# A hybrid attention and retention layer: 96 stores go to ScalarE's queue, gated rows are fetched in two groups, and the retention's projection begins with two first halves

## The chip, the cores and the metric

The kernel runs on one core of a Trainium2 chip. The time is that of one execution on the device in microseconds (us); each kernel is run several times and the median is taken. One execution is also recorded by the hardware profiler. Its span runs from the first to the last instruction. PE is TensorE (PEld its weight loads), DVE is VectorE, ACT is ScalarE, POOL is GpSimd, SP is SyncE, which does nothing here but issue transfers; "SPq" in a row is that queue.

## The reference

One layer of a diffusion backbone over 1024 latent tokens of width 1024 (with 256 context tokens), in fp32. The input is modulated and normalized to `hx`; one input projection feeds a 2-D neighbourhood attention (8 heads of 64), a bidirectional chunkwise retention (4 heads, 128 for queries and keys, 256 for values) and gates. What the change touches comes after both:

```python
def _ret_output(o, g):
    of = o.astype(jnp.float32)
    mu = jnp.mean(of, axis=-1, keepdims=True)
    var = jnp.mean(jnp.square(of - mu), axis=-1, keepdims=True)
    on = ((of - mu) * lax.rsqrt(var + EPS)).astype(o.dtype)
    return _merge_heads(on) * jax.nn.silu(g)

def _merge(o_na, o_ret, gate_na, gate_ret, w_proj_na, w_proj_ret, w_out):
    merged = jax.nn.sigmoid(gate_na) * (o_na @ w_proj_na) + jax.nn.sigmoid(gate_ret) * (o_ret @ w_proj_ret)
    return merged @ w_out
...
x = x + g1 * _merge(o_na, o_ret, xga, xgb, w_proj_na[l], w_proj_ret[l], w_out[l])
x = x + g2 * _conv_ffn(hx2, w_up[l], conv_w[l], conv_b[l], w_down[l])
```

## The kernel before

Every fp32 operand is split in two parts, `hi` (a cast on ScalarE) and `lo` (the source less `hi`, on VectorE), and a product takes three matmuls: hi x hi, hi x lo, lo x hi. Tiles are 128 partitions x 512 elements. Everything is kept transposed: a block `db` of 128 channels stands on the partitions, and the tokens are two halves of 512. The stages follow one another in this order, with their places in the trace: start and modulation (0 to 90 us), neighbourhood attention with the heads' projections (90 to 390), retention (to 720), `pn`, the projection of the attention's output (720 to 774), Gates (774 to 926), `pr`, the projection of the retention's output (929 to 1025), `om`, the output projection (to 1118), and the ConvFFN (to the end).

In neighbourhood attention and retention, some gate products run in between ("filled in"): `gate_fill` copies the product from PSUM to `gs` on ScalarE and stores it to DRAM, `d_gate` (L361). In the retention, `mix_c` transposes a head's output by PE, copies it to `ot` on ScalarE, and stores it to `d_oret` (L1210). In the `pn` stage a product times its gate goes to `pnt` and is stored to `d_pn` (L1509).

The class `Gates` (a seven-product scheme for 2x2 blocks, hence `Seven`) computes the remaining gates. A unit is a retention head ("ret") or a block of merge gates ("merge"). `done` applies the activation to the product on ScalarE, multiplies by the fetched `o` on VectorE (not for the second block of a merge unit), and stores the tile `c` to `d_orr` (the gated rows of retention's output), `d_pn` or `d_gate` (L1487). The units run interleaved, in a list `steps` of pairs (unit, product); each step is 12 matmuls, `u` in the rows. The last unit has ten list places from its own first step, `n0`, to the end.

The gated rows come back from `d_orr` for `pr`: `orr_raw(half, k)` gives the tiles and issues the load of one (k of 8, half of 2), and `split` makes the two parts of it. Their tiles take the places of parts of `hx`, so that a load's split must stand behind the last product that reads that part. Loads that must be split go through `rawload`, which has three buffers named `raw`; split weights have six buffers named `wc`. `merge_load` brings the merge gates and the `pn` products into `sg`; `g = pr * gate + pn` is then split to `mh`, `ml` for `om`.

What sets the order: the framework's scheduler sets the order of each engine's instructions from the program's order and dependencies; `late` and the manual parts pin it. Each engine, and each queue, takes its instructions strictly in this order; all loads and stores of this kernel are issued by SP. A store whose tile isn't ready thus holds the loads behind it.

Of the kernel before, what the change touches and what calls it, by code (L numbers as in the profile page):

```python
# [9 lines left out]
F32R = mybir.dt.float32r  # L10
AF = mybir.ActivationFunctionType
ALU = mybir.AluOpType
# [6 lines left out]
KB = D // P  # L19
# [10 lines left out]
RH = 4  # L30
# [10 lines left out]
def tile_hybrid_layer(ctx, tc: tile.TileContext, io, dbg=None):  # L41
    nc = tc.nc
    vec, act, pool, pe, sync = nc.vector, nc.scalar, nc.gpsimd, nc.tensor, nc.sync
# [41 lines left out]
    def split(hi, lo, src, lo_eng=None):  # L85
        act.copy(hi, src)  # L86
        (lo_eng or vec).tensor_tensor(lo, src, hi.bitcast(F32), ALU.subtract)  # L87
# [28 lines left out]
    def mm_a(out, wcs, hi, lo):  # L116
        for _ in chain(out, wcs, hi, lo):
            pass
# [235 lines left out]
    def gate_fill(p, tag, bufs, g, wg):  # L354
        db, br = g
        for half in range(2):
            m = mm_tile()
            yield from chain(m, wg, hxs(0, half), hxs(1, half), STEP)
            t = p.tile([P, 512], F32, tag=tag, bufs=bufs, name="gs")
            act.copy(t, m)  # L360
            sync.dma_start(d_gate[db * 2 + br, half], t)  # L361
            if half:
                spilled[g] = True
            yield
# [701 lines left out]
    class Head:  # L1066
# [129 lines left out]
        def mix_c(self, n):  # L1196
            tb, o = self.back[n], self.o[n]
            tp = prt.tile([P, 2, P], F32, tag="s", bufs=2, name="tpo")
            for b in range(2):
                pe.transpose(tp[:, b], o[:, b * P : (b + 1) * P], ident)  # L1200
            h = self.h
            end = h == RH - 1 and n >= NTB - 2
            if end:
                ot = wpool.tile([P, 512], F32, tag="raw", bufs=3, name="oe")[:, : 2 * P].rearrange("p (b t) -> p b t", b=2)
            else:
                ot = rt.tile([P, 2, P], F32, tag="ot", bufs=2, name="ot")
            act.copy(ot, tp)
            stores.append((d_oret[2 * h : 2 * h + 2, :, tb * P : (tb + 1) * P].rearrange("b p t -> p b t"), ot))
            if not end:
                sync.dma_start(*stores.pop())  # L1210

    stores = []

# [117 lines left out]
    def g_ps(name):  # L1331
        return pg.tile([P, 512], F32, tag="g", bufs=6, name=name)
# [26 lines left out]
        sync.dma_start(raw, d_onat[n * P : (n + 1) * P])  # L1359
        onr.append(raw)  # L1360
    while stores:
        sync.dma_start(*stores.pop(0))
    for n, raw in enumerate(onr):
        tp = pg.tile([P, NPAIR, P], F32, tag="g", bufs=6, name="tpn")
        for k in range(NPAIR):
# [76 lines left out]
    class Gates(Seven):  # L1442
# [38 lines left out]
        def done(self, b, half, t=None, src=None):  # L1481
            t = self.c[b, half]
            src, n, cs = t if src is None else src, self.n, slice(half * 512, half * 512 + 512)
            act.activation(t, src, AF.Silu if self.kind == "ret" else AF.Sigmoid)
            if self.kind == "ret" or b == 0:
                vec.tensor_tensor(t, t, self.o, ALU.mult)
            sync.dma_start(d_orr[2 * n + b, :, cs] if self.kind == "ret" else d_pn[n, half] if b == 0 else d_gate[2 * n + 1, half], t)  # L1487

    nsp = len(spilled) // 2
    gu = [Gates("ret", h) for h in range(RH)] + [Gates("merge", db) for db in range(nsp, KB)]  # L1490
# [1 line left out]
    for db in range(KB):  # L1492
        if db % 2 == 0:
            hs = hx_sums(db // 2)
            next(hs)
        wp = [wload(io["w_pna"][db, 0])]
        for half in range(2):
            sl_ = slice(half * 512, half * 512 + 512)
            m = g_ps("pn")
            mm_a(m, wp, lambda k: ona[0][:, k, sl_], lambda k: ona[1][:, k, sl_])  # L1500
            t = onap.tile([P, 512], F32, tag="pn", bufs=3, name="pnt")
            if (db, 0) in spilled:
                g = onap.tile([P, 512], F32, tag="sg", bufs=2, name="sgt")
                sync.dma_start(g, d_gate[2 * db, half])
                act.activation(g, g, AF.Sigmoid)
                vec.tensor_tensor(t, m, g, ALU.mult)
            else:
                act.copy(t, m)
            sync.dma_start(d_pn[db, half], t)  # L1509
        if db % 2 == 0:  # L1510
            next(hs)
    gu[0].load()
# [16 lines left out]
    orr = {}  # L1529

    def orr_raw(half, k):
        i, kb = (k // KH if half else 1 - k // KH), k % KH + KH * half
        orr[half, k] = [hxpool.tile([P, 512], F32R, tag=f"{t}{i}{kb}", bufs=1, name="orr") for t in ("high", "low")]
        return orr[half, k], rawload(d_orr[k, :, half * 512 : half * 512 + 512], late)

    gate_sums = down_sums(gr, RET_SUMS, GATE_SUMS)
    steps = interleaved(0, len(gu))
    n0, fetched = steps.index((len(gu) - 1, 0)), None
    for n, (i, k) in enumerate(steps):
        gu[i].step(k)  # L1540
        if n % 3 == 1:
            next(gate_sums, None)
        if fetched:
            split(*fetched[0], fetched[1])
            fetched = None
        if n0 <= n < n0 + 2 * RH:
            fetched = orr_raw(0, n - n0)
    wp0 = [wload(io["w_pret"][0, i]) for i in range(2)]
    for _ in gate_sums:
        pass  # L1550
    gr.release()
# [6 lines left out]
    def gtile(half, dt, name):  # L1558
        return gpool[half].tile([P, 512], dt, tag="g", bufs=2 * KB + 1, name=name)

    sg = {}

    def merge_load(db, halves=(0, 1)):
        for half in halves:
            sg[db, 0, half] = gtile(half, F32, "sg")
            sync.dma_start(sg[db, 0, half], d_pn[db, half])
            sg[db, 1, half] = t = gtile(half, F32, "sg")
            sync.dma_start(t, d_gate[2 * db + 1, half])
            if (db, 1) in spilled:
                act.activation(t, t, AF.Sigmoid)  # L1570
# [8 lines left out]
    pjp = sb("out_sums", "right")  # L1579
    out_sums = down_sums(pjp, GATE_SUMS, NH, 7)  # L1580
    mg = {}
    wp_next = wp0
    for db in range(KB):
        wp = wp_next
        if db == 0:
            merge_load(0, (0,))
            for k in range(2 * RH):
                hl, raw = orr_raw(1, k)
                split(*hl, raw)
            merge_load(0, (1,))  # L1590
        if db + 1 < KB:
            wp_next = [wload(io["w_pret"][db + 1, i]) for i in range(2)]
            merge_load(db + 1)
        if db == 2:
            brow(0, gate1)
        for half in range(2):
            m = g_ps("pr")
            mm_a(m, wp, lambda k: orr[half, k][0], lambda k: orr[half, k][1])
            g = sg[db, 1, half]
            vec.tensor_tensor(g, m, g, ALU.mult)  # L1600
            (vec if db == KB - 1 else pool).tensor_tensor(g, g, sg[db, 0, half], ALU.add)
            h_, l_ = gtile(half, F32R, "mh"), gtile(half, F32R, "ml")
            split(h_, l_, g)
            mg[db, half] = (h_, l_)
            if db > 1:
                next(out_sums, None)
    pjp.release()
    wo = {}
    for kb in range(KB):
# [475 lines left out]
```

## Time and profile before

| | before |
|---|---|
| runs, us | 1777.6, 1780.02, 1781.48 (median 1780.02) |
| span of the profiled execution, us | 1772.4 |
| median of the runs less that span, us | 7.6 |
| PE busy | 1725.5 us, 97% |
| DVE, ACT, POOL busy | 74%, 48%, 32% |
| DMA engines | 44.3% of the span, 262 MB |
| mean granted clock of PE | 0.991 |

The profiled execution's own time isn't listed apart from the runs; its span is, and the runs lie 5.2 to 9.1 us above it. The profile's busy times say how much of the span each engine worked; the trace's rows give an instruction's start, its length, its engine and line, and in brackets the idle time before it and what ended that idle time. A row of waits has the total, the number of times and the longest wait.

### The profile page before, as it was taken

How to read it: one execution, taken by the hardware profiler on the slowest of the kernel's cores; microseconds unless marked ns; L12 is line 12 of the kernel's file. 1: busy time of each engine (PE TensorE's matmuls, PEld its weight loads, DVE VectorE, ACT ScalarE, POOL GpSimd, SP SyncE). 2: the span in 40 equal slices, each digit the busy share in tenths (PEclk: the TensorE clock that was granted, in tenths of full speed). 3: DMA queues.
4: the chain of work that ended last, by engine and by line, in shares of the span. 5: the costliest groups of instructions: out<-in, count | busy, mean ns of one | idle time of the engine just before them, and what ended most of it. 6: DMA issues, size and time to landing. Idle time of an engine off the chain costs nothing.

```text
span 1772.4 us, 24732 instructions
## 1 busy us (share of the span) xinstructions
PE 1725.5 (97%) x8357; PEld 1429.4 (81%) x8357; DVE 1312.3 (74%) x2458; ACT 851.1 (48%) x1833; POOL 570.9 (32%) x477
## 2 busy tenths in 40 slices
PE   8799999999999999999999999999999999999997
PEld 4588888888888888788877888888888888788886
DVE  5978888765776766777655556889899999876755
ACT  5667666652443444443444323454444444554444
POOL 2610000002334343555412400155455555211444
PEclk9899999999999999999999999999999999999999
DMA  9133334432231212677548733742322332586754
GB/s 357 56 113 120 106 113 134 142 110 104 72 108 48 72 39 65 202 243 241 187 168 278 236 127 137 253 147 91 117 90 89 119 119 90 167 297 191 241 167 151
DMA packets 139552, 261.62 MB, mean 148 GB/s; under 512 B 15872, under 2 KB 28320, under 8 KB 139424
## 3 DMA queue, kind: packets, MB, share of 16 engines
q1 hardware_dynamic: 139424, 260.03, 44.3%
q8 instruction: 66, 1.08, 0.3%
q14 instruction: 62, 0.51, 0.1%
HBM read 187.87 MB, written 69.48 MB: 145 GB/s over the span
## 4 chain that ended last, share of the span: by engine, by line
PE 39%; issue 6%; DVE 5%; DMA 3%; POOL 3%; ACT 1%; SPq 0%; POOLq 0%; DVEq 0%; ACTq 0%
PE u L1374 27%; PE y L1374 4%; PE pr L111 2%; PE pr L112 1%; PE pr L110 1%; PE om L123 1%; PE om L122 1%; PE om L121 1%; DMA raw<-d_orr 1%; DVE wc L87 1%; POOL x L1899 0%; DMA uu<-d_t 0%; DMA ur<-in_w_up 0%; DVE b L1350 0%; POOL pd L1936 0%
## 5 line engine op out<-in xcount | busy, mean ns | idle before, releaser
L1374 PE MATMUL u<-T,wc 128*128 128x512 f32 x960 | 225.7, 391 | 0.6 <-ACT pu L1413 0.3
L1374 PE MATMUL y<-wc,ahl 128*128 128x512 f32 x924 | 212.0, 391 | 2.9 <-DVE wc L87 1.8
L1374 PEld LDWEIGHTS u<-T,wc 128*128 128x128 f32 x960 | 179.4, 188 | 41.5 <-ACT pu L1413 4.2
L1374 PEld LDWEIGHTS y<-wc,ahl 128*128 128x128 f32 x924 | 174.4, 189 | 40.2 <-DVE wc L87 2.5
L87 DVE TENSOR_TENSOR wc<-ur,wc 128x512 fp32r<-128x512 f32 x137 | 125.0, 915 | 62.2 <-ACT wc L86 62.2
L86 ACT CAST wc<-ur 128x512 fp32r<-128x512 f32 x137 | 85.1, 622 | 124.3 <-PE y L1374 71.8
L111 PE MATMUL mm<-low,wc 128*128 128x512 f32 (+1 forms) x328 | 124.0, 378 | 0.0
L1374 PE MATMUL u<-h2a,wc 128*128 128x512 f32 x480 | 112.4, 389 | 0.7 <-DVE pu L1422 0.7
L110 PE MATMUL mm<-hx,wc 128*128 128x512 f32 x264 | 107.4, 407 | 0.3 <-DVE vc L221 0.3
L1374 PEld LDWEIGHTS u<-h2a,wc 128*128 128x128 f32 x480 | 90.0, 188 | 19.9 <-DVE pu L1422 1.2
L112 PE MATMUL mm<-hx,wc 128*128 128x512 f32 x264 | 105.1, 398 | 0.0
L86 ACT CAST wc<-s 128x512 fp32r<-128x512 f32 x80 | 49.6, 621 | 89.7 <-PE u L1374 86.9
L123 PE MATMUL mm<-wc,low 128*128 128x512 f32 (+1 forms) x240 | 91.2, 380 | 0.0
L1513 POOL TENSOR_TENSOR col<-col,bcol 128x32 f32<-128x32 f32 x1 | 0.3, 254 | 281.9 <-DVE aw L538 281.9
L1374 PE MATMUL u<-hxT,wc 128*128 128x512 f32 x384 | 89.6, 389 | 0.0
L87 DVE TENSOR_TENSOR wc<-s,wc 128x512 fp32r<-128x512 f32 x80 | 87.3, 1092 | 3.1 <-ACT wc L86 2.6
L1374 PEld LDWEIGHTS u<-hxT,wc 128*128 128x128 f32 x384 | 72.1, 188 | 15.0
L87 DVE TENSOR_TENSOR wc<-raw,wc 128x512 fp32r<-128x512 f32 x92 | 71.4, 784 | 13.3 <-ACT wc L86 13.2
L121 PE MATMUL mm<-wc,hx 128*128 128x512 f32 x192 | 75.2, 392 | 0.6 <-ACT r L1105 0.6
L122 PE MATMUL mm<-wc,hx 128*128 128x512 f32 x192 | 75.2, 392 | 0.0
L86 ACT CAST wc<-raw 128x512 fp32r<-128x512 f32 x92 | 57.0, 622 | 32.3 <-DMA raw<-in_w_up 5.0
L111 PEld LDWEIGHTS mm<-low,wc 128*128 128x128 f32 x328 | 62.1, 189 | 6.9
(393 smaller groups left out, 4695.7 us busy)
## 6 DMA issues: line engine op xcount, KB each, us to landing
ur<-in_w_up SPq DMA_DIRECT2D x80, 256.0 KB, 3.0
ur<-d_a SPq DMA_DIRECT2D x77, 256.0 KB, 3.0
aw<-in_w_ada SPq DMA_DIRECT2D x32, 512.0 KB, 3.3
pj<-in_w_down SPq DMA_DIRECT2D x44, 256.0 KB, 4.9
d_w<-pj SPq DMA_DIRECT2D x44, 256.0 KB, 2.0
d_a<-sa SPq DMA_DIRECT2D x44, 256.0 KB, 2.0
ur<-d_w SPq DMA_DIRECT2D x44, 256.0 KB, 3.5
d_a<-at SPq DMA_DIRECT2D x33, 256.0 KB, 2.7
```

What stands on the lines that cost most here:

```text
L86: act.copy(hi, src)
L87: (lo_eng or vec).tensor_tensor(lo, src, hi.bitcast(F32), ALU.subtract)
L110: pe.matmul(out, wh, xh, start=k == 0, stop=False)
L111: pe.matmul(out, wh, xl, start=False, stop=False)
L112: pe.matmul(out, wl, xh, start=False, stop=k == n - 1)
L121: pe.matmul(out, ah, bh, start=first, stop=False)
L122: pe.matmul(out, ah, bl, start=False, stop=False)
L123: pe.matmul(out, al, bh, start=False, stop=last)
L1374: pe.matmul(out, a, b, start=first and n == 0, stop=last and n == 2, skip_group_check=True)
L1513: pool.tensor_tensor(col[:, 16:48], col[:, 16:48], bcol[:, 16:48], ALU.add)
```

## The change

Three things change. First, the stores of L361, L1210, L1362, L1487 and L1509 (16 + 30 + 2 + 32 + 16 = 96) are issued by ScalarE instead of SP. Second, the gated rows of half 0, which were fetched one by one at the last unit's list places 0 to 7, are fetched at places -6 to -3 (k = 0 to 3) and 1 to 4 (k = 4 to 7), the first two of half 1 at places 7 and 9, and `w_pret` of block 0 is loaded within the last three list places. Third, `pr` runs in the order (0,0), (1,0), (0,1), (1,1), (2,0), (2,1) and on, as (block, half); the weights of block 1 are loaded before the six rows of half 1 that are left.

```diff
             act.copy(t, m)
-            sync.dma_start(d_gate[db * 2 + br, half], t)
+            act.dma_start(d_gate[db * 2 + br, half], t)
...
             if not end:
-                sync.dma_start(*stores.pop())
+                act.dma_start(*stores.pop())
...
     while stores:
-        sync.dma_start(*stores.pop(0))
+        act.dma_start(*stores.pop(0))
...
-            sync.dma_start(d_orr[2 * n + b, :, cs] if self.kind == "ret" else d_pn[n, half] if b == 0 else d_gate[2 * n + 1, half], t)
+            act.dma_start(d_orr[2 * n + b, :, cs] if self.kind == "ret" else d_pn[n, half] if b == 0 else d_gate[2 * n + 1, half], t)
...
-            sync.dma_start(d_pn[db, half], t)
+            act.dma_start(d_pn[db, half], t)
...
-    n0, fetched = steps.index((len(gu) - 1, 0)), None
+    n0, fetched, wp0 = steps.index((len(gu) - 1, 0)), None, []
+    fetches = {d: (k // 8, k % 8) for k, d in enumerate((-6, -5, -4, -3, 1, 2, 3, 4, 7, 9))}
...
-        if n0 <= n < n0 + 2 * RH:
-            fetched = orr_raw(0, n - n0)
-    wp0 = [wload(io["w_pret"][0, i]) for i in range(2)]
+        if n - n0 in fetches:
+            fetched = orr_raw(*fetches[n - n0])
+        if n >= len(steps) - 3 and len(wp0) < 2:
+            wp0.append(wload(io["w_pret"][0, len(wp0)]))
+    split(*fetched[0], fetched[1])
...
-    wp_next = wp0
-    for db in range(KB):
-        wp = wp_next
-        if db == 0:
-            merge_load(0, (0,))
-            for k in range(2 * RH):
+    wps = {0: wp0}
+    merge_load(0, (0,))
+    for n, (db, half) in enumerate(((0, 0), (1, 0), (0, 1), (1, 1), *((db, half) for db in range(2, KB) for half in range(2)))):
+        nx = 1 if n == 0 else db + 1
+        if nx < KB and nx not in wps:
+            wps[nx] = [wload(io["w_pret"][nx, i]) for i in range(2)]
+            if nx > 1:
+                merge_load(nx)
+        if n == 0:
+            for k in range(2, 2 * RH):
                 hl, raw = orr_raw(1, k)
                 split(*hl, raw)
+            merge_load(1)
             merge_load(0, (1,))
```

The order on SP at the end of Gates, before (names are `out<-in` with a running number; `d_orr` loads are the gated rows, `in_w_pret` the weights of `pr`, `o` a fetch for the gates):

```order
L1487 DMA d_pn_62<-c_10135 128x512
L91 DMA raw_10144<-d_orr_63 128x512
L91 DMA raw_10171<-d_orr_63 128x512
L1479 DMA o_10221<-d_pn_62 128x512
L1487 DMA d_gate_61<-c_10162 128x512
L1487 DMA d_pn_62<-c_10190 128x512
L91 DMA raw_10198<-d_orr_63 128x512
L91 DMA raw_10243<-in_w_pret 128x512
L1487 DMA d_gate_61<-c_10215 128x512
L91 DMA raw_10248<-in_w_pret 128x512
L1566 DMA sg_10269<-d_pn_62 128x512
L1568 DMA sg_10271<-d_gate_61 128x512
```

And the same place on SP after the change:

```order
L91 DMA raw_10134<-d_orr_63 128x512
L1479 DMA o_10181<-d_pn_62 128x512
L91 DMA raw_10204<-d_orr_63 128x512
L91 DMA raw_10206<-in_w_pret 128x512
L91 DMA raw_10232<-in_w_pret 128x512
L1479 DMA o_10237<-d_pn_62 128x512
L91 DMA raw_10261<-d_orr_63 128x512
L91 DMA raw_10286<-in_w_pret 128x512
L91 DMA raw_10291<-in_w_pret 128x512
L91 DMA raw_10298<-d_orr_63 128x512
L1569 DMA sg_10281<-d_pn_62 128x512
L1571 DMA sg_10283<-d_gate_61 128x512
```

The stores are gone from it, the weights of two blocks stand ahead of most of half 1's rows, and two of those rows (`raw_10204`, `raw_10261`) stand ahead of block 1's weights.

PE at the end of the first chain of `pr` (24 matmuls), before, and then after:

```order
L112 MATMUL pr_10347<-orr_10196,wc_10250 128x512
L110 MATMUL pr_10378<-orr_10274,wc_10245 128x512
L111 MATMUL pr_10378<-orr_10275,wc_10245 128x512
L112 MATMUL pr_10378<-orr_10274,wc_10245 128x512
L110 MATMUL pr_10378<-orr_10280,wc_10245 128x512
```

```order
L112 MATMUL pr_10347<-orr_10132,wc_10234 128x512
L110 MATMUL pr_10398<-orr_9883,wc_10288 128x512
L111 MATMUL pr_10398<-orr_9884,wc_10288 128x512
L112 MATMUL pr_10398<-orr_9883,wc_10288 128x512
L110 MATMUL pr_10398<-orr_9905,wc_10288 128x512
```

Before, the second chain reads new rows (half 1) with the same weights; after, it reads the rows of half 0 once more, with block 1's weights.

ScalarE in the retention, before, and then after (`ot` is the copy of a head's transposed output, `v` the cast of projected values):

```order
L1125 CAST qk_5448<-tp_5445 128x256
L1207 COPY ot_5454<-tpo_5451 128x256
L1100 CAST v_5463<-mm_5391 128x256
L1134 ACTIVATE kz_5579<-r0_5466,dec_158 128x128
L1156 COPY ds_5489<-dS_5476 128x256
```

```order
L1125 CAST qk_5448<-tp_5445 128x256
L1207 COPY ot_5454<-tpo_5451 128x256
L1210 DMA d_oret_58<-ot_5454 128x2x128
L1100 CAST v_5463<-mm_5391 128x256
L1134 ACTIVATE kz_5579<-r0_5466,dec_158 128x128
```

The store now stands between the copy and the next cast on ScalarE.

More of the change, by code (lines that the diff above doesn't have):

```diff
@@ L1581, in tile_hybrid_layer @@
     mg = {}
-    wp_next = wp0
-    for db in range(KB):
-        wp = wp_next
-        if db == 0:
-            merge_load(0, (0,))
-            for k in range(2 * RH):
+    wps = {0: wp0}
[8 more added lines that the diff above has]
+            for k in range(2, 2 * RH):
                 hl, raw = orr_raw(1, k)
                 split(*hl, raw)
+            merge_load(1)
             merge_load(0, (1,))
[L1591 to L1594, printed above, removed]
+        if (db, half) == (2, 0):
             brow(0, gate1)
[L1596 to L1606, printed above, removed]
+        m = g_ps("pr")
+        mm_a(m, wps[db], lambda k: orr[half, k][0], lambda k: orr[half, k][1])
+        g = sg[db, 1, half]
+        vec.tensor_tensor(g, m, g, ALU.mult)
+        (vec if db == KB - 1 else pool).tensor_tensor(g, g, sg[db, 0, half], ALU.add)
+        h_, l_ = gtile(half, F32R, "mh"), gtile(half, F32R, "ml")
+        split(h_, l_, g)
+        mg[db, half] = (h_, l_)
+        if db > 1:
+            next(out_sums, None)
     pjp.release()
```

## The prediction

> **What bounds the kernel now.** I read the page's totals, then the waits of PE between the retention and the output projection, then PE's row of instructions through that stretch, and last SP's and ScalarE's rows for who makes it wait.
>
> ```profile
> span 1772.4 us, 24732 instructions
> PE 1725.5 (97%) x8357; PEld 1429.4 (81%) x8357; DVE 1312.3 (74%) x2458; ACT 851.1 (48%) x1833; POOL 570.9 (32%) x477
> ```
>
> PE is busy for 97% of the span, so a change that takes no matmul away can win only what PE loses: idle gaps, and matmuls that run slowly after them. The change touches 720 to 1025 us, and PE's waits from 640 to 1040 are these:
>
> ```profile
> PE pr L110 <- ACT wc L86: 2.8, 1, 2.8
> PE pn L112 <- DVE wc L87: 2.2, 2, 1.5
> PE pr L110 <- ACT orr L86: 2.1, 3, 1.3
> PE tpn L1366 <- DVE ona L1369: 2.1, 1, 2.1
> PE pr L111 <- DVE orr L87: 1.4, 4, 0.7
> ```
>
> Three of the five belong to pr, the retention's projection, which waits for splits (the cast on ACT, the difference on DVE) of weights and gated rows: 6.3 us. PE's timeline gives the pace and the gaps:
>
> ```profile
> 904.45 8.32 PE L1374 MATMUL u<-hxT,wc 128*128 128x512 f32 x36
> 912.61 0.39 PE L1374 MATMUL u<-hx,wc 128*128 128x512 f32 x1
> ...
> 925.99 0.39 PE L1374 MATMUL u<-hx,wc 128*128 128x512 f32 x1
> 929.18 0.50 PE L110 MATMUL pr<-orr,wc 128*128 128x512 f32 x1 [2.80 <-ACT wc L86]
> ...
> 931.78 0.63 PE L110 MATMUL pr<-orr,wc 128*128 128x512 f32 x1
> 932.20 0.63 PE L111 MATMUL pr<-orr,wc 128*128 128x512 f32 x1
> ...
> 939.82 0.50 PE L111 MATMUL pr<-orr,wc 128*128 128x512 f32 x1 [0.72 <-DVE orr L87]
> ...
> 944.44 0.50 PE L110 MATMUL pr<-orr,wc 128*128 128x512 f32 x1 [1.27 <-ACT orr L86]
> ...
> 1025.09 0.39 PE L112 MATMUL pr<-orr,wc 128*128 128x512 f32 x1
> 1025.31 0.39 PE L121 MATMUL om<-wo,mh 128*128 128x512 f32 x1
> ```
>
> Undisturbed, 36 matmuls start within 912.61 - 904.45 = 8.16 us, 0.2267 us apart; at 931.78 the step to the next is 0.42. The granted clock explains the slow ones:
>
> ```profile
> 929.20:932.60 3.40, 3.40 (x8) 2.42 (x9) 2.04 (x5) 2.33 (x4) 0.00 (x0) 0.59 0.83 288
> 946.30:949.70 3.40, 3.18 (x7) 2.10 (x8) 2.08 (x4) 1.24 (x2) 0.65 (x1) 0.59 0.72 253
> 949.70:1010.00 60.30, 60.30 (x266) 49.94 (x266) 31.93 (x42) 21.96 (x37) 23.94 (x18) 1.00 0.78 263
> ```
>
> (After the length: busy time and count of PE, PEld, DVE, ACT, POOL, then clock, DMA share and GB/s.) Twice the clock is 0.59 for 3.40 us; from 949.70 PE is full at clock 1.00, so nothing is left to win there, though DMA is at 0.78.
>
> The sum available: from the last Gates matmul (925.99) to the first of the output projection (1025.31) are 99.32 us, and 1 + 384 matmuls (8 blocks x 2 halves x 24) at 0.2267 take 87.3. The excess is **12.05 us**: 6.3 in the eight gaps, 2 x 3.40 x (1 - 0.2267/0.42) = 3.1 by the half clock, and the other 2.6 in slow restarts behind the gaps (0.50 instead of 0.39 long).
>
> Why the rows come late is on SP's row, in the waits of its queue, and in the chain:
>
> ```profile
> 917.64 0.32 SPq L1487 DMA_DIRECT2D d_pn<-c  x1
> 918.06 0.88 SPq L91 DMA_DIRECT2D raw<-d_orr  x2
> ...
> 923.27 0.32 SPq L1487 DMA_DIRECT2D d_pn<-c  x1
> 923.64 0.43 SPq L91 DMA_DIRECT2D raw<-d_orr  x1
> ```
>
> ```profile
> SPq L1487 <- DVE c L1486: 15.3, 5, 4.7
> SPq L91 <- DVE orr L87: 11.1, 9, 2.0
> ```
>
> ```profile
> 916.92 0.70 DVE c L1486
> ...
> 929.24 2.60 DMA raw<-d_orr
> 931.85 0.63 ACT orr L86
> 932.50 0.70 DVE orr L87
> ...
> 940.69 4.85 DMA raw<-d_orr
> ```
>
> Loads of gated rows go out right behind stores that sat at the head of SP's queue until VectorE's product was there: 15.3 us between 890 and 950. (In the chain: a load's way to its landing, 2.60 to 4.85 us, then 0.63 of cast and 0.70 of difference.) Half 0's last load leaves at 923.64 and half 1's eight between 929.24 and 940.69, while pr(0, half 1) would at full pace want them from 934.6 to 939.4 (929.18 + 24 x 0.2267, then 0.68 each).
>
> **The change, part by part.**
>
> *Stores off SP.* 96 issues leave SP; the 64 of the other lines are loaded again only a stage later and free queue time alone, while the 32 of L1487 free the loads behind them, by up to the 4.7 us of the longest wait. The price is that ScalarE now issues them, in order, and its next cast stands behind each.
>
> ```profile
> L1210 SPq DMA_DIRECT2D d_oret<-ot x30: 360/371/386, 475.7 to 711.6; - x30
> ```
>
> ```profile
> L91 SPq DMA_DIRECT2D raw<-in_w_ret x32: 327/328/1362, 315.4 to 601.2; - x32
> ```
>
> ```profile
> 475.26 0.38 ACT L1207 COPY ot<-tpo 128x256 f32<-128x256 f32 x1
> 476.60 0.37 ACT L1100 CAST v<-mm 128x256 fp32r<-128x256 f32 x1 [0.96 <-PE mm L123]
> ```
>
> ```profile
> ACT v L1100 <- PE mm L123: 32.8, 30, 2.7
> ```
>
> In the retention a store of 0.37 follows ot's copy, where ScalarE is idle for 0.96 us until PE delivers mm; from 450 to 700 the cast v waits so 30 times, 1.09 us in the mean: hidden. No row shows an issue from ScalarE; I bound it by 0.36 (SP's fastest for this transfer) and 1.36 (SP's slowest of a load in the same stage), which would cost 30 x (1.36 - 1.09) = 8 us. I take SP's median of 0.37, the same transfer, so 0 on PE. In the attention stage ten stores of d_gate stand between a copy and casts with no gap:
>
> ```profile
> 340.63 1.08 ACT L495 CAST PT<-ptp 128x512 fp32r<-128x512 f32 x2
> ...
> 344.71 0.76 PE L511 MATMUL R<-PT,V 128*128 128x256 f32 x5
> ```
>
> At most 10 x 0.37 = 3.7 us, at least 0. I take 0: the casts end at 341.71 and the product that reads PT starts at 344.71, so 3.0 us, less VectorE's difference of 0.7, cover it. In the Gates stage each store also waits for the product that follows its own activation, 0.70 on VectorE and what is queued there:
>
> ```profile
> ACT wc L86 <- PE u L1374: 45.8, 27, 2.1
> ```
>
> ```profile
> 740.00:775.00 35.00, 33.85 (x148) 27.65 (x149) 33.43 (x40) 17.99 (x34) 15.83 (x10) 1.00 0.64 203
> ```
>
> There ScalarE's weight casts wait 45.8 us (775 to 926) for buffers that PE has not yet freed: they run ahead of PE, and that lead covers 32 stores at 0.37 + 0.70 (34 us, spread over the 151 us of the stage). If the lead were gone, the next late thing would be wc of a Gates product. In the w_pna stage (740 to 775) DVE is busy 33.43 of 35 us and its lateness sets PE's 2.2 us of waits; ScalarE's 16 stores there neither feed nor free DVE: 0, between -2.2 and +1.6 (a half clock from one new gap).
>
> *Gated rows in two groups, w_pret early.* The same 16 + 4 loads, no instruction more. The first four of half 0 come 6 steps before the last unit's first step (2.72 us of 12 matmuls each), the others from one step after, so half 0 is split by the end of Gates instead of the cast at 928. The 2.80 gap at 929.18 goes, with its half clock (1.6) and its restart. The splits, 0.63 on ScalarE and 0.70 on VectorE each, are only moved to earlier steps; ScalarE has the room there (the 45.8 us above).
>
> *Two first halves first.* pr(1, half 0) now stands before pr(0, half 1), 24 x 0.2267 = 5.44 us more until half 1 is wanted. With pr starting at 926.2, pr(1, 0) starts at 931.7 and pr(0, 1) at 937.1; its pairs follow every 0.68 us, the last at 941.9. New is that block 1's weights are wanted at 931.7 instead of at the third chain. Both of its loads go out before the six remaining rows, near 925 (an estimate: behind half 0's last load of before, 923.64, and two issues); with 0.4 of issue, a landing of 2.60 to 4.85 and 1.3 of split the first is ready by 929.3 to 931.6: hidden, barely in the worst case; the second is wanted 2.7 later. The six rows have three buffers, so two rounds of issue 0.4 + landing + 1.3: from 927, 2 x (0.4 + 2.6 + 1.3) = 8.6, or 2 x (0.4 + 4.85 + 1.3) = 13.1, so the last is ready between 935.6 and 940.1, or up to 3 later if SP's interleaved sg loads and one more round of weights stand between (943.1). Need: 941.9. Leftover: 0 to 1.2 us of gap, and with a half clock and a restart up to 3.6. I take 1.0.
>
> A rule to weigh here: "TensorE: Matmul & The Clock Gate" of the Trainium skill, section "What's actually happening", has the clock halved after at least one idle window of about 3.4 us, the windows running freely. The trace agrees with the 3.40 us and half rate, but shows it behind a 2.80 us gap and again behind scattered gaps of 1.27 and less. By the rule a leftover gap of 1.2 would cost 1.2 and the sum would be 10.8; by the row up to 3.6, and 8.4.
>
> *Downstream.* The loads of w_out are paced by PE and by buffers, the stage behind is full: it moves along unchanged, gain and all.
>
> The sum: 0 (stores) - 12.05 + 1.0 = **-11.0 us**. The profiled execution spans 1772.4; the runs' median, 1780.02, is 7.6 above that, which I take as outside the span and unchanged. Forecast 1780.02 - 11.0 = 1769.0. No change means within 0.2%, 3.6 us, about what a measurement of this kernel can tell from none.
>
> **The rivals.**
>
> *Half 1 is still late* (faster, by about half). For: only three raw buffers, a wait of 11.1 us on SP for them (DVE orr), DMA share 0.72 to 0.83 and a landing of 4.85. Against: 5.44 us more time, two rows fetched before. A gap of 3 at pr(0, 1) with one half clock (1.6) and restarts (1.4) leaves 6.0 of 12.05: 1774.
>
> *ScalarE's queue becomes the bound* (slower). Place: the retention, where a store of ot stands ahead of the cast v, whose waits give it 1.09 us each. Price 30 x (issue - 1.09) us. It cancels the gain from an issue of 1.09 + 11/30 = 1.46 us, and passes +0.2% from 1.58; at 2.0 it is 27.3 - 11.0 = +16.3, 1796. Against: 0.37 on SP for the same transfer.
>
> *The change doesn't do what it says*: the rows are late by the raw buffers alone (11.1 beside 15.3 on SP), so the six rows of half 1 are no earlier and the gaps move from 929 to 937. Time 1780, within 1777 to 1783. Against: half 0 alone has the 2.80 gap and its half clock, and it no longer uses buffers then. The Trainium skill's page "DMA: Bandwidth & Descriptors", section "Issuing engines are not separate DMA queues", speaks for this rival: all issuers share 16 engines, and only sequencer time is saved. By it alone the stores are worth 0. The trace's 15.3 us of waiting at the head of SP's queue is a cost of another kind.
>
> **How the numbers follow.** Gaps gone: 0.70, 1764 to 1771. Half 1 late: 0.16, 1771 to 1776.5, 0.02 of it within 0.2%. No effect: 0.08. ScalarE the bound: 0.06, all slower. Faster 0.70 + 0.14 = 0.84, same 0.10, slower 0.06. The low end is all of 12.05 and the 2.2 in the w_pna stage, less half the spread of the runs (1777.6 to 1781.48): 1780.0 - 12.05 - 2.2 - 1.9 = 1764; the high end is the late half, 1774, with a little over the same half spread: 1776.5.
>
> **What would show it.** Right: no d_orr load behind a store on SP; the first pr matmul within 0.3 us of the last u; no PE wait over 0.5 us for orr or wc up to 950; clock 1.00 from 926 to 950; 87 to 89 us from the last u to the first om. Stores: issues of 0.3 to 0.4 us on ScalarE, and PE's waits in attention, retention and Gates as before. Wrong: a gap at pr(0, 1) with clock 0.59 behind it; PE waits for v, PT or wc that come behind a store; or a stage before 720 that is longer by more than a microsecond.

## The result: 12.6 us faster, nearly all of it where PE had waited, and more than one part of the change needed the others

| | before | after |
|---|---|---|
| median of the runs, us | 1780.75 (1777.6 to 1782.48, 4 runs) | 1768.2 (1766.18 to 1771.13, 4 runs) |
| ratio, with 95% interval | | 0.9929 [0.9909, 0.9948] |
| span of the profiled execution, us | 1772.4 | 1768.2 |
| that execution's own time, us | not listed | 1769.98 |

A ratio of 0.9929 is 12.6 us of 1780.75 (9.3 to 16.2 by the interval). Forecast was 1769.0. The two first profiles alone show only 4.2 us of it; the next section says where the rest is.

The page after, its first lines and its queues:

```profile
span 1768.2 us, 24667 instructions
PE 1722.8 (97%) x8357; PEld 1429.4 (81%) x8357; DVE 1305.5 (74%) x2458; ACT 851.4 (48%) x1833; POOL 571.0 (32%) x477
...
q1 hardware_dynamic: 121504, 239.05, 41.2%
q10 hardware_dynamic: 17920, 20.98, 3.4%
```

Every engine has as many instructions in the page as before (the program's total is 65 lower, of 24732); 21 MB now go through a second queue, q10, ScalarE's. PE's waits from 640 to 1040 us had five rows, and have two:

```profile
PE tpn L1366 <- DVE ona L1369: 2.1, 1, 2.1
PE pn L112 <- DVE wc L87: 1.4, 1, 1.4
```

The three rows of pr are gone. PE's timeline at the two ends of pr:

```profile
927.42 0.39 PE L1374 MATMUL u<-hx,wc 128*128 128x512 f32 x1
927.64 0.39 PE L110 MATMUL pr<-orr,wc 128*128 128x512 f32 x1
...
1014.46 0.39 PE L112 MATMUL pr<-orr,wc 128*128 128x512 f32 x1
1014.68 0.39 PE L121 MATMUL om<-wo,mh 128*128 128x512 f32 x1
```

From the last Gates matmul to the first of om are 1014.68 - 927.42 = 87.26 us, which is the 87.27 that 385 matmuls need at full pace: not one is late. The same stretch of time in the two kernels, before and then after (length, busy time and count of PE, PEld, DVE, ACT, POOL, then PE's clock, DMA share, GB/s):

```profile
926.00:1025.00 99.00, 92.67 (x385) 73.60 (x384) 54.00 (x73) 39.30 (x66) 30.41 (x22) 0.97 0.74 248
```

```profile
926.00:1025.00 99.00, 99.00 (x438) 81.91 (x438) 51.88 (x76) 36.96 (x63) 30.50 (x22) 1.00 0.77 258
```

In 99 us PE now does 438 matmuls and not 385, at clock 1.00.

### The profile page after: what moved, and what is told of

Its sections match the earlier page's. It is cut to its first block, busy times and chain, and to the rows that moved or that the text cites. A ratio compares the mean times of both kernels' runs of the same rounds, so it can differ in the third digit from the quotient of the medians.

```text
span 1768.2 us, 24667 instructions
## 1 busy us (share of the span) xinstructions
PE 1722.8 (97%) x8357; PEld 1429.4 (81%) x8357; DVE 1305.5 (74%) x2458; ACT 851.4 (48%) x1833; POOL 571.0 (32%) x477
## 4 chain that ended last, share of the span: by engine, by line
PE 44%; issue 5%; POOL 3%; DVE 3%; DMA 1%; ACT 1%; SPq 0%; POOLq 0%; ACTq 0%; DVEq 0%
PE u L1374 29%; PE y L1374 4%; PE pr L111 2%; PE pr L110 2%; PE pr L112 2%; PE om L121 1%; PE om L123 1%; PE om L122 1%; POOL x L1903 1%; PE pn L112 1%; PE pn L110 1%; PE pn L111 1%; DMA vo<-d_h 1%; DVE wc L87 0%; DMA uu<-d_t 0%
## 5 line engine op out<-in xcount | busy, mean ns | idle before, releaser
L87 DVE TENSOR_TENSOR wc<-wr,wc 128x512 fp32r<-128x512 f32 x56 | 54.2, 972 | 21.7 <-ACT wc L86 21.5
```

## Where the time lies, by stage and kernel

The lengths below are differences between first matmuls in each kernel's profiled execution: attention and retention (first R to first tpn), w_pna stage (first tpn to first Gates u), Gates with pr (to the first om), up projection (its first u to the first y, the down projection). S is "stores on ScalarE", F "fetch in two groups with early w_pret", P "two first halves first".

| kernel | parts | ratio to before [95%] | attention, retention | w_pna | Gates + pr | up | span |
|---|---|---|---|---|---|---|---|
| before | none | | 600.28 | 53.76 | 251.52 | 421.50 | 1772.4 |
| e1, before again | none | 0.9987 [0.9972, 1.0003] | 600.17 | 54.24 | 251.34 | 426.99 | 1780.9 |
| after | S F P | 0.9929 [0.9909, 0.9948] | 600.33 | 52.76 | 239.46 | 427.88 | 1768.2 |
| e9, after again | S F P | 0.9931 [0.9915, 0.9947] | 600.12 | 52.80 | 239.47 | 421.57 | 1763.1 |
| e2 | S | 1.0004 [0.9986, 1.0021] | 600.53 | 52.78 | 255.86 | 425.86 | 1780.5 |
| e3 | F P | 1.0042 [1.0026, 1.0059] | 599.98 | 53.67 | 257.05 | 426.92 | 1786.7 |
| e5 | F P, pr pinned | 1.0027 [1.0014, 1.0040] | 599.87 | 54.82 | 255.60 | 426.50 | 1785.4 |
| e4 | S F | 0.9958 [0.9942, 0.9973] | 600.18 | 52.81 | 243.59 | 422.50 | 1767.5 |
| e11 | S P | 0.9956 [0.9942, 0.9971] | 600.58 | 52.76 | 244.58 | 422.88 | 1768.0 |
| e6 | F P, S for L1487 only | 0.9938 [0.9920, 0.9956] | 600.43 | 54.09 | 239.46 | 421.97 | 1764.0 |
| e7 | S F P, ot stored 5 times | 1.0003 [0.9990, 1.0016] | 610.97 | 55.69 | 239.46 | 425.79 | 1780.6 |
| e8 | S F P, convolution late | 0.9917 [0.9900, 0.9934] | 600.26 | 52.78 | 239.46 | 422.48 | 1764.7 |
| e10, e8 again | as e8 | 0.9926 [0.9912, 0.9941] | 600.04 | 52.79 | 239.47 | 423.00 | 1762.5 |

Three things stand in it. Gates with pr repeats to 0.2 us in the same kernel and is 12 us shorter after the change. The w_pna stage is 52.8 in all kernels that store pnt from ScalarE and 53.7 to 54.8 in those that store it from SP (e7's 55.7 is apart: its stage began late). The up projection, which no part of the change touches, is about 422 or about 427, in the same kernel (after: 427.88 and 421.57; before: 421.50 and 426.99). The first profile of before had caught a short one and that of after a long one: so the spans differ by 4.2 and the medians by 12.6. What makes it short or long stands at e8. The start, up to the first R, isn't in the table; it takes 119.76 and 121.96 us in before, 122.13 and 123.49 in after. No part of the change touches it, and e3 and e5, which leave the stores on SP, have 121.12 and 122.72.

## The experiments

**e1, before once more**, with no edit.

> The kernel before once more, unchanged, for a second profile of it. The profile on record spans 1772.4 us, while its timed runs lie at 1777.6 to 1782.5 and those of the changed kernel lie only 1.8 us above their spans. Theory (the prediction's: the 7.6 us lie outside the span): run less span is again near 7.6 us. Rival (the first profile caught an unusually short execution): run less span is 1.8 us, the span is 1776 to 1781, and the extra 4 to 8 us stand in a stage that the change doesn't touch, most likely at the first T products of the up projection, where the changed kernel's profile has gaps of 1.55 and 2.60 us and this one had 0.28. In both the stretch from the last Gates matmul to the first of om takes 99.3 us, 12 over the full pace. Ratio 1.000 within 0.002.

The median of 12 runs is 1777.38 (1773.29 to 1782.7), and the profiled one took 1782.7 with a span of 1780.9: 1.8 us lie outside the span, as after the change, not 7.6. The rival holds. The first 721 us were 2 us longer this time, and the up projection 5.5, by the waits that the changed kernel had there too (rows at e8).

**e2, only the stores move**, all five lines as in the change; the first of them:

```diff
-            sync.dma_start(d_gate[db * 2 + br, half], t)
+            act.dma_start(d_gate[db * 2 + br, half], t)
...
```

> Only the 96 stores move to ScalarE; fetch places and the order of pr stay. Theory (the stores free the loads behind them, the places of the fetches and the order bring the rest): the last half 0 rows and w_pret come 1 to 2 us earlier, half 1's eight rows are still held by three buffers and wanted from 934, so 3 to 5 of the 12 us go: 99.3 becomes 94 to 96.5 us, ratio 0.997 to 0.998. Rival A (the wait at the head of SP's queue was all of it): 87 to 89 us, ratio 0.993. Rival B (ScalarE's queue pays): stages before 774 us or the Gates stage longer by 2 us or more, ratio 1.000 or above. By the Trainium skill's page on DMA (DMA: Bandwidth & Descriptors, Issuing engines are not separate DMA queues) the move saves only issue time on SP and brings nothing on PE: 99.3.

The ratio is 1.0004: no gain. From the last Gates matmul (934.10) to om (1030.34) it takes 96.2 us, 3 less than before, as the theory had it, but Gates itself became 7.4 longer (159.63 from its first to its last matmul, before 152.19). By these signs it is rival B, whose cause the rows below put more exactly. PE's waits from 770 to 1045:

```profile
PE u L1374 <- DVE pu L1422: 4.5, 1, 4.5
PE pr L110 <- ACT orr L86: 3.3, 3, 2.3
PE pr L111 <- DVE orr L87: 0.7, 3, 0.2
```

The first row is new. Its way back goes from VectorE to ScalarE to SP; the three timelines:

```profile
919.61 0.69 DVE L87 TENSOR_TENSOR orr<-raw,orr 128x512 fp32r<-128x512 f32 x1 [3.25 <-ACT orr L86]
...
925.27 0.69 DVE L1422 TENSOR_TENSOR pu<-u,pu 128x512 f32<-128x512 f32 x1
```

```profile
918.96 0.62 ACT L86 CAST orr<-raw 128x512 fp32r<-128x512 f32 x1 [3.35 <-DMA raw<-d_orr]
```

```profile
914.59 0.32 SPq L1479 DMA_DIRECT2D o<-d_pn  x1
915.00 0.38 SPq L91 DMA_DIRECT2D raw<-d_orr  x1
```

The load of a gated row left SP only behind `o`, the fetch for the next Gates product, which waits for a buffer that VectorE frees. With the stores off SP, another instruction waits at its head. The row's cast then held ScalarE for 3.35 us and its difference VectorE for 3.25, and behind it in VectorE's order stands `pu`, which PE needs. (By the chain that ended last, `c`, its activation and store on ScalarE, and the first split of `w_pret` stand between the two.) The load isn't later than before: it is the last row of half 0, which there left SP at 923.64, 8.6 us later. But there its split stood behind the last `pu` of Gates, and in this kernel's order it stands ahead of it. The wait has moved from a queue that only delays pr to two engines that feed Gates.

**e3, only the fetch and the order of pr**: the changed kernel with all 96 stores back on SP, by five lines like this one:

```diff
-            act.dma_start(d_orr[2 * n + b, :, cs] if self.kind == "ret" else d_pn[n, half] if b == 0 else d_gate[2 * n + 1, half], t)
+            sync.dma_start(d_orr[2 * n + b, :, cs] if self.kind == "ret" else d_pn[n, half] if b == 0 else d_gate[2 * n + 1, half], t)
...
```

> The fetch in two groups, early w_pret and the two first halves first, with all 96 stores on SP as before. Theory: the first chains find their rows and weights, so the 2.80 us gap goes; the six rows of half 1 stand behind the last stores of Gates on SP (about 925 and 930) and come 2 to 3 us later than in the full change, a gap of 1 to 2 us at pr(0, half 1) with one half clock: 99.3 becomes 89.5 to 92.5 us, ratio 0.9945 to 0.9965. Rival (the stores are worth nothing): 87 to 88 us, ratio 0.993 as the full change. Rival (the head of the queue decides): 95 us or more.

It is slower than before, 1.0042, with Gates and pr at 257.05; the nearest to it was the rival by which the head of the queue decides. PE's timeline:

```profile
921.54 0.39 PE L1374 MATMUL u<-hx,wc 128*128 128x512 f32 x1
928.90 0.80 PE L110 MATMUL pr<-orr,wc 128*128 128x512 f32 x1 [6.97 <-ACT wc L86]
929.49 5.42 PE L1374 MATMUL u<-hxT,wc 128*128 128x512 f32 x12
```

The scheduler had put the first matmul of pr ahead of the last 12 of Gates, so that the moved matmul could be the cause, and not the stores. e5 takes that away.

**e5, as e3, with the first chain of pr pinned behind Gates on PE.**

```diff
...
-        mm_a(m, wps[db], lambda k: orr[half, k][0], lambda k: orr[half, k][1])
+        for _ in chain(m, wps[db], lambda k: orr[half, k][0], lambda k: orr[half, k][1], pin=late if n == 0 else lambda ins: ins):
+            pass
```

> As the order-only kernel (fetch in two groups, early w_pret, two first halves first, stores on SP), but the first chain of pr is pinned to its place behind the last Gates matmul on PE; in the order-only kernel the scheduler had put one pr matmul ahead of the last 12 of Gates, and these waited with it for 6.97 us. Theory A (that wait was the store at the head of SP's queue: the last half 0 row went out at 923.73 behind it, and the casts queued behind that row's cast on ScalarE): the wait stays, 5 to 8 us, behind the last Gates matmul or ahead of it, plus half clocks, and the Gates stage and pr together take 253 to 257 us (order-only 257.1, before 251.3 to 251.5, the full change 239.5). Theory B (the moved matmul was the cause): the wait is 0 to 1.5 us and the two stages take 240 to 245. By the Trainium skill's page on DMA (issuing engines are not separate queues, only issue time is saved) B as well.

Theory A: 255.60 us, ratio 1.0027, and the wait stays, now in front of Gates' own matmul. PE, ScalarE and SP:

```profile
932.11 4.83 PE L1374 MATMUL u<-hxT,wc 128*128 128x512 f32 x12 [7.56 <-ACT wc L86]
```

```profile
930.30 0.62 ACT L86 CAST orr<-raw 128x512 fp32r<-128x512 f32 x1 [5.07 <-DMA raw<-d_orr]
930.92 0.62 ACT L86 CAST wc<-raw 128x512 fp32r<-128x512 f32 x1
931.44 0.61 ACT L86 CAST wc<-wr 128x512 fp32r<-128x512 f32 x1
```

```profile
925.99 0.32 SPq L1487 DMA_DIRECT2D d_pn<-c  x1
926.35 0.43 SPq L91 DMA_DIRECT2D raw<-d_orr  x1
```

To be read from below: the row's load goes out behind a store that waited for its product; the cast of the row holds ScalarE for 5.07 us; behind it stands `wc<-wr`, the weights of the last Gates products, and PE waits 7.56 us for them (and 3.5 us for weights once more in pr). The early fetch puts the casts of the rows into Gates, among the casts that PE waits for. That costs nothing if the rows land in time; if they do not, PE waits for the store's product, the landing and the casts. So stores on ScalarE are worth 255.6 - 239.5 = 16.1 us of Gates and pr when F and P are there (e6 shows that 32 of them suffice), and cost 4.4 (255.86 - 251.5) when they come alone.

**e4, stores and fetch, old order of pr** (and with it block 1's weights again behind half 1's rows). Against the changed kernel:

```diff
-    for n, (db, half) in enumerate(((0, 0), (1, 0), (0, 1), (1, 1), *((db, half) for db in range(2, KB) for half in range(2)))):
+    for db in range(KB):
...
+        for half in range(2):
...
```

> The stores on ScalarE and the early fetch with w_pret, but pr in the order of before, (0,0), (0,1), (1,0) and on. Theory: no 2.80 us gap, but half 1 is wanted from 931.7 on, when its rows come between 930 and 938: gaps of 3 to 5 us in sum at pr(0, half 1) with one or two half clocks, so 92 to 96 us from the last Gates matmul to the first of om, ratio 0.995 to 0.998. Rival (the order of pr brings nothing, since the stores and the fetch suffice): 87 to 88 us, ratio 0.993.

Gates and pr take 243.59 us, 7.9 less than before (e1 and before: 251.34 and 251.52); from the last u to om 91.4, a little under the theory's 92 to 96. The order of pr is worth the other 4.1. Half 1's rows come a little late, by PE's timeline (the longest of three gaps; the others are 0.23 and 0.22):

```profile
939.14 0.50 PE L110 MATMUL pr<-orr,wc 128*128 128x512 f32 x1 [1.14 <-ACT orr L86]
```

```profile
936.60:940.00 3.40, 1.80 (x6) 0.74 (x6) 2.10 (x4) 1.92 (x4) 0.00 (x0) 1.00 0.93 316
940.00:943.40 3.40, 3.40 (x9) 2.61 (x10) 1.81 (x3) 1.92 (x4) 0.30 (x1) 0.50 0.88 289
```

The gaps are 1.59 us together, and the 4.1 us are those, the 3.40 us at clock 0.50 behind them (1.7 lost), and 0.8 that is left over and that I put down to slower restarts.

**e11, stores and order of pr, old fetch.** Against the changed kernel:

```diff
...
-        if n - n0 in fetches:
-            fetched = orr_raw(*fetches[n - n0])
-        if n >= len(steps) - 3 and len(wp0) < 2:
-            wp0.append(wload(io["w_pret"][0, len(wp0)]))
-    split(*fetched[0], fetched[1])
+        if n0 <= n < n0 + 2 * RH:
+            fetched = orr_raw(0, n - n0)
+    wp0 = [wload(io["w_pret"][0, i]) for i in range(2)]
...
-            for k in range(2, 2 * RH):
+            for k in range(2 * RH):
```

> The stores on ScalarE and the order with two first halves, but the fetch and the first w_pret loads as before (half 0 at the last unit's places 0 to 7, then all eight rows of half 1). It leaves out the one part that the other kernels held. Theory (with the rows fetched as before, ScalarE's and VectorE's splits of half 0 stand in Gates and wait for their loads, as in the stores-only kernel, whose Gates stage had a gap of 4.65 us, and half 1 has eight rows to bring instead of six): Gates and pr together 246 to 253 us, ratio 0.996 to 1.001. Rival (order and stores suffice): 239.5 to 241, ratio 0.993.

It takes 244.58 us, a little under the theory's range; 5.1 over the full change. PE's longest wait there is e2's:

```profile
PE u L1374 <- DVE pu L1422: 3.5, 1, 3.5
```

pr itself has no wait. So F keeps the splits from holding up Gates; F is both the rows' places and the early `w_pret`, and no run takes these two apart. With P, half 1 is in time even with eight rows; but Gates ended 5.1 us later here, which gave the rows as much more time, so that P alone would do isn't shown.

**e6, only the 32 stores of L1487 on ScalarE**, with F and P: the other four lines of stores are back on SP, the first of them:

```diff
-            act.dma_start(d_gate[db * 2 + br, half], t)
+            sync.dma_start(d_gate[db * 2 + br, half], t)
...
```

> The full change, but of the 96 stores only the 32 of the Gates stage (L1487) are on ScalarE; the 64 of d_gate, d_oret and d_pn from the other stages stay on SP. Theory (the 64 cost and bring nothing): Gates and pr together 239 to 241 us, ratio to before 0.992 to 0.995, no wait of PE for orr or wc. Rival (the 64 matter, by SP's queue in the w_pna stage or by the scheduler's order): 243 or more, or a stage before 774 us that differs by over 2 us.

The ratio is 0.9938 and Gates with pr 239.46: those 32 carry the gain there. The rival has a small part: the w_pna stage is 54.09 against 52.8, in line with the other kernels that store pnt from SP. The chain that ended last, in before, has the reason:

```profile
750.66 0.69 DVE pnt L1506
751.36 0.33 SPq L1509
751.78 3.74 DMA sgt<-d_gate
755.61 0.64 ACT sgt L1505
756.28 0.69 DVE pnt L1506
```

The load of the next gate, sgt, stood behind pnt's store on SP, and VectorE's work behind that. After the change the chain that ended last runs over PE alone from 745 to 775. The 64 other stores are worth 0.9 to 2.1 us by the table.

**e7, each ot tile stored five times from ScalarE**, four of them to memory that nothing reads.

```diff
...
             if not end:
                 act.dma_start(*stores.pop())
+                for d in d_extra:
+                    act.dma_start(d[2 * h : 2 * h + 2, :, tb * P : (tb + 1) * P].rearrange("b p t -> p b t"), ot)
```

> The full change with four more stores of each ot tile on ScalarE, to scratch memory that nothing reads (30 x 4 issues): a store place in the retention then costs 5 x 0.366 = 1.83 us of ScalarE instead of 0.366. It prices the rival that ScalarE's queue becomes the bound. By the prediction's formula PE pays 30 x (1.83 - 1.09) = 22 us, ratio to before about 1.005. Theory (ScalarE has other idle time behind the cast, and PE other matmuls to run, so the 1.09 is a lower bound of the room): 0 to 12 us, ratio 0.993 to 1.000. If the room were only the wait at the single place: 30 us and more.

Attention and retention took 610.97 us, 10.6 more, and the w_pna stage 2.9 more, since its first inputs came late (a wait for ona of 5.7 us, 2.1 without). Ratio 1.0003 against 0.9929: 13 us, in all a little over the theory's 12. The extra issues, and PE's longest wait:

```profile
L1213 ACTq DMA_DIRECT2D d_extra<-ot x120: 366/502/1532, 478.1 to 728.8; - x120
```

```profile
PE tpn L1369 <- DVE ona L1372: 5.7, 1, 5.7
```

Each extra issue, in a row of five, takes not 0.366 but 0.53 us in the mean (63.4 us for 120), so ScalarE was held for 63 us more; PE paid 10.6 of it in the retention. The prediction's formula would have charged 30 x (0.37 + 4 x 0.53 - 1.09) = 42.

**e8 and e10, a version meant to beat both: the convolution of the second plain block later.** In the changed kernel's first profile the up projection had these waits of PE, 1110 to 1200 us (e1, which is the kernel before, had the same two rows with 2.6 and 1.2):

```profile
PE u L1374 <- ACT pu L1413: 2.6, 1, 2.6
PE u L1374 <- DVE wc L87: 1.6, 1, 1.6
```

```diff
...
-        act.activation(ta, ta, AF.Silu)
+        pin(act.activation(ta, ta, AF.Silu))
...
-        conv(j, *us2)
+        if n == 0:
+            conv(j, *us2)
     units[PLAIN + 1].load()
-    for i, n in interleaved(PLAIN, NF):
+    for s, (i, n) in enumerate(interleaved(PLAIN, NF)):
         units[i].step(n)
+        if s == 1:
+            conv(seq[PLAIN - 1], *us2, late)
```

(The first of VectorE's two pieces is pinned in the same way.)

> The full change, and in the up projection the convolution of the second plain block (its VectorE pieces and its Silu) pinned behind the second step of the first seven-product unit, so that the copy of pu on ScalarE and the splits of wc on VectorE stand ahead of it; PE's order is the same. Theory (these two queue places make the gaps of 1.55 and 2.60 us at the first T products, and the half clock behind them): the up stage from its first u to the first y takes 421 to 423 us instead of 427.9, ratio to before 0.989 to 0.992 and about 3 us under the full change in the median. Rival (VectorE's work there is the bound in any order, or PSUM comes free later): the gaps move behind the T products, 425 to 429 us, no gain.

> The changed kernel once more, beside the two that follow, for its own spread. Theory (only the stretch from Gates to om changed, and the other differences of the first profiles are from run to run): that stretch is 239.5 us again, attention and retention 600.2 to 600.5, the up stage from its first u to the first y either about 422 or 426 to 428. Ratio 0.992 to 0.995. Rival (the up stage is longer because of the change): always 427 to 428.

> The kernel with the late convolution once more, on the same chip as the changed kernel, to tell the two apart. Theory (the gaps at the first T products are gone whatever their DMA times): the up stage 421 to 423 us, median 2 to 4 us under the changed kernel, ratio to before 0.990 to 0.9925. Rival (the first time it was run to run): no difference within 1 us, or an up stage of 426 to 428.

With it the two waits are 0.2 and none in both profiles, and another of 0.9 for pu from VectorE is new (e8's rows):

```profile
PE u L1374 <- DVE pu L1422: 0.9, 1, 0.9
...
PE u L1374 <- ACT pu L1413: 0.2, 1, 0.2
```

The up projection takes 422.48 and 423.00. But the changed kernel has 421.57 in e9, without any of these waits, so only its long executions can gain; and e9 refutes its rival, that the change makes the stage longer. What differs is how VectorE's splits of T (combined inputs of the seven-product scheme) and GpSimd's sums for the next weights meet (L1389 is the first of these). VectorE's and GpSimd's timelines in the changed kernel's long execution, and then in e9:

```profile
1149.61 7.60 DVE L87 TENSOR_TENSOR T<-uu,T 128x512 fp32r<-128x512 f32 x7
1149.57 1.29 POOL L1389 TENSOR_TENSOR s<-s,ur 128x512 f32<-128x512 f32 x1 [11.90 <-DMA ur<-in_w_up]
```

```profile
1149.73 4.30 DVE L87 TENSOR_TENSOR T<-uu,T 128x512 fp32r<-128x512 f32 x7
1150.07 5.12 POOL L1389 TENSOR_TENSOR s<-s,ur 128x512 f32<-128x512 f32 x1 [11.03 <-DMA ur<-in_w_up]
```

Either three of VectorE's splits take 1.8 us instead of 0.69 while GpSimd's three sums run, or GpSimd's first sum takes 5.1 to 5.5 us and no split is slow. All six long executions without the edit are of the first kind (e2 with one slow split, the others with three), all five short ones of the second. What decides it isn't shown. It isn't how early the loads come: from the stage's first u to GpSimd's first sum it is 39.3 to 42.9 us in the long executions and 40.4 to 42.0 in the short ones. e10 had three slow splits as well, and neither of the two waits over 0.2: there the late convolution did what it was meant to do. On one chip the medians are 1765.0 (1763.81 to 1767.03) and 1766.91 (1762.1 to 1768.08), 1.9 us apart where 2 to 4 were expected, ratios to before 0.9926 and 0.9931 with intervals that overlap widely. That it is faster than the changed kernel isn't shown.

## Why the prediction was right, and where its steps were not

**The sum.** It took 12.05 us of excess, less 1.0 for a leftover gap. Gates with pr went from 251.52 (251.34) to 239.46: 12.06 (11.88), with no leftover. The w_pna stage gave 1.0 to 1.5 more, so the stages add up to about 13 us where 11.0 were forecast. That the median of 1768.2 came within 1 us of the forecast is in part luck, with runs that spread over about 5 us. The leftover was too careful. Block 1's weights went out not near 925 but here, by SP's timeline after:

```profile
919.07 0.33 SPq L1479 DMA_DIRECT2D o<-d_pn  x1
919.50 0.37 SPq L91 DMA_DIRECT2D raw<-d_orr  x1
919.98 2.09 SPq L91 DMA_DIRECT2D raw<-in_w_pret  x2
```

They were split by 926.91 and wanted at 933.08. The last row of half 1 was split here, on VectorE:

```profile
939.70 0.69 DVE L87 TENSOR_TENSOR orr<-raw,orr 128x512 fp32r<-128x512 f32 x1
```

It was ready at 940.39 and wanted at 943.28. The estimate for two rounds, 935.6 to 940.1, was nearly right (pr began 1.4 us later than estimated); the 3 us on top of it, which gave the leftover, didn't come.

**"The stores free the loads behind them."** Right in what it does: with the stores alone the last row of half 0 leaves SP 8.6 us earlier (e2). Wrong in how, since SP waits at its head nearly as long as before, 38.7 us from 890 to 950 in all its rows and 42.8 before. Of the stores' waits the prediction had one row, 15.3 us; this is the other, and below it the one that took their place:

```profile
SPq L1487 <- ACT c L1484: 5.1, 4, 2.4
```

```profile
SPq L1479 <- DVE c L1486: 15.1, 3, 8.9
```

15.1 us for the fetch of `o` took the place of 20.4 for the stores; in e2, too, a row stood behind that fetch. The gain comes from where the loads now stand between such waits, and that needs S and F together: F without S loses 4 us or more (e3, e5), S without F loses 4 (e2) or, with P, keeps 7 of 12 (e11). The prediction took the excess as one term, but its reasons give the 2.80 us gap to F and the time for half 1 to P, as if each had a price of its own; they don't. The cost of S alone, and that F and P alone are slower than before, were in none of its rivals.

The rule of the Trainium skill that was set beside the third rival ("DMA: Bandwidth & Descriptors", section "Issuing engines are not separate DMA queues": another issuer saves only the time of the issue) would make S worth nothing. With F and P there, S for the 32 stores of L1487 is worth 16 us, from e5 (none) to e6 (these alone); e5's pinned chain is the only other difference, and without it (e3) the gain is larger. What the rule leaves out is what waits behind a waiting issue.

**ScalarE pays nothing.** Right. Attention and retention are 600.28 and 600.33. The issue takes what it took on SP:

```profile
L1210 ACTq DMA_DIRECT2D d_oret<-ot x30: 366/366/806, 478.2 to 714.0; - x30
```

In Gates ScalarE's casts do wait behind stores now, 13.2 us, and behind late rows 12.0 (7.0 before); its lead over PE, 45.8 before, pays for it, with 35.2 left (its waits from 775 to 928):

```profile
ACT wc L86 <- PE u L1374: 35.2, 24, 2.1
ACT wc L86 <- DVE c L1486: 13.2, 8, 2.6
ACT orr L86 <- DMA raw<-d_orr: 12.0, 7, 6.1
```

The slower rival's price was mis-sized: e7 paid 10.6 us in the retention where its formula gives 42. So ScalarE makes up most of a delay at the cast of v before PE needs it.

**The w_pna stage at 0.** A small miss: 0.9 to 2.1 us were gained, inside the bounds given. The step that failed is that these stores "neither feed nor free DVE" and "free queue time alone": on SP they held the load of sgt, and VectorE waited for that (e6).

**"7.6 us lie outside the span."** Wrong, and harmless for the difference: 1.8 us do (1769.98 and 1768.2). The other 5.8 are that the profiled execution of before was a short one.

**The clock.** The forecast bound of 3.6 us for a leftover gap went by the row, not by the rule. e4 bears the row out: 1.59 us of gaps, none over 1.14, brought 3.40 us at clock 0.50, and the loss was 4.1. The rule (an idle window of about 3.4 us, in the Trainium skill's "TensorE: Matmul & The Clock Gate", "What's actually happening"), taken literally, gives 1.6 there, and the trace doesn't agree with it. PE was busy for 1.80 of the 3.40 us ahead of the half clock, so a window about half idle was enough here. (The 0.59 of the prediction's two rows is a mean: they begin 0.6 us ahead of the half clock, which is 0.50 from 929.82 to 933.23 and from 946.89 to 950.30.)

**A sign of being wrong** appeared, a stage before 720 that is over 1 us longer: the start took 2.4 us more in the first profile of after. As said at the table, it differs about as much between two executions of one kernel.

## What to carry to other kernels

A queue or an engine that works in order passes a wait on to whatever stands behind: when a waiting instruction is taken from one, look at which one waits at its head next, and at what the late data's consumers hold up on their own engines. Parts of such a change are not to be priced one by one; the value of one is set by whether the others bring the data in time. And before a span is set against a median, take a second profile: here two executions of one kernel differed by 8.5 us in spans, in stages that the change did not touch.

## What was not expected of the hardware

Issues in a row from ScalarE's queue take longer than single ones: 0.53 us in the mean and up to 1.53 (e7), against 0.366. PE's half clock comes in windows of 3.41 us, one in some places (e4, before) and two in others (three once, in e3), as behind the two gaps of 1.55 and 2.60 us in the changed kernel's up projection:

```profile
1161.35:1164.76 3.41, 2.36 (x6) 1.88 (x7) 3.41 (x5) 1.51 (x4) 0.00 (x0) 0.50 0.62 190
1164.76:1168.17 3.41, 3.41 (x10) 2.64 (x9) 1.60 (x3) 0.24 (x1) 3.05 (x2) 0.50 0.49 181
```

Here PE was idle at the start of the first window (2.36 of 3.41 us busy) and the half clock went on for a second; in e4 and before PE was busy for 3.28 us or more of the first, and no second came. One place is against so simple a rule (e1 at 946.25, 3.31 us busy and still a second), so what makes it one or two stays open. For the first half window the 13 profiles agree from 130 to 1700 us: every window at full clock with PE busy for at most 1.69 of its 3.41 us was followed by one at half clock, none with over 2.02, and between them it went both ways.
